# First two weight blocks computed together, input block by input block, and the first token group left unnormalised

## The chip, the cores and the metric

The kernel runs on one core of a Trainium2 chip. The metric is the device time of one launch in microseconds (us), the median of several runs. One run was also taken with the hardware profiler. The engines are named as the profile names them: PE (TensorE, matmuls; PEld its weight loads), DVE (VectorE), ACT (ScalarE), POOL (GpSimd) and SP (SyncE, which issues nearly all transfers).

## What is computed

One layer of a decoder for 2048 prompt tokens and 8 sequences of 8 sample tokens (2112 tokens in all), width 1024, in float32:

```
h    = rmsnorm(x) * norm_mix_w                       # one factor per token, rs = rsqrt(mean(x*x) + eps)
proj = h @ w_in                                      # 1024 x 4096: rq rk rv rg | hq hf hi hg, 4 heads of 128 each
o_r  = retention(rotary(rq), rotary(rk), rv)         # chunkwise, decay per head
o_h  = hgrn2(silu(hq), f(hf), hi)                    # chunkwise, decay per element from the forget gate f
o    = concat(head_rmsnorm(o_r)*silu(rg), head_rmsnorm(o_h)*silu(hg))
x    = x + o @ w_out
x    = x + square(relu(rmsnorm(x) @ w_up)) @ w_down
y    = rmsnorm(x)                                    # and the final states of both recurrences
```

The factor `rs` is one number per token, so a product of unnormalised tokens with the weights, multiplied by `rs` behind the product, is the same value as the product of normalised tokens.

## The kernel before

Tokens are kept transposed, 128 channels by tokens. They are mixed in three groups (`GROUPS`: 640, 768 and 704 tokens); the two recurrences of a group are worked head by head (`mix`), and a second phase, the MLP, follows for the whole. Only the start of the first group matters here.

Every float32 operand of a product is split into a high part in PE's fp32r type (`hi`, an ACT copy) and the rest (`lo`, a DVE subtraction). A product is three matmuls, hi-hi, hi-lo and lo-hi. With 640 tokens the group has two `pieces` of 320 columns. A projection block is 128 output channels: 8 input blocks (`KB`) x 3 x 2 pieces = 48 matmuls of 320 columns into two PSUM banks. A weight unit (`unit`, 128x1024) holds the eight 128x128 weights of one such block.

PSUM is split into two pools of four banks: `pj` for projections and `mm` for the mixing work. The order of the small work is laid down by an agenda: `at` and `later` put functions on it, and `tick` runs what is due each time `matmul` has issued a certain number of columns. `flush` runs the whole agenda.

`norm_start` reads the first group's 8 input blocks (`x_block`, 128x640) and splits `x * norm_mix_w` into hi and lo; there `rs` is not applied. It computes the squares (L600), their sum (L603) and by `factor` (L647, L407, L408) the token factor `rs`. While `g.post` is true, `normed` multiplies products by `rs` (L760). In head 0 of this group (`start` in `project`), blocks hf and hq (`sg`, `z`) are copied out of PSUM unnormalised (`evacuated`, L782); block three (rq) and block four (rk) stay in PSUM until rotary products L843 take them with tables that hold `rs` already (L817); then come the two gate blocks, and `values`, which multiplies tokens (as the stationary side) by the value weights and copies them out (L875). Between these, `norm_rest` has all 8 input blocks scaled by `rs` (L705) and split once more (L708, L712); from `values` of head 0 on, the normalised blocks are used.

`norm_squares`, for the next group, reads the next group's input into `ld` buffers (`ld<-x`, 128x768). It runs on the agenda of head 3, but its four first reads need nothing but free buffers, and they stand near the front of SP's queue.

Of the kernel before, what the change touches and what calls it, by code (L numbers as in the profile page):

```python
# [27 lines left out]
C = 128  # L28
# [24 lines left out]
W_BP = 0  # L53
# [141 lines left out]
class Kernel:  # L195
# [187 lines left out]
            out.append(self.blocks.popleft())  # L383
        return out

    def proj(self, g, blocks, acts):

        if self.singles:
            out = [(self.bank()[:, :c1 - c0], c0, c1) for c0, c1 in g.pieces]
# [227 lines left out]
    def norm_start(self, g):  # L617

        nc, T = self.nc, g.T
        self.starts(g)  # L620
        g.post, g.x = True, []
        for kb in range(KB):
            x, hi, lo = self.x_block(g, kb, True), self.getr(), self.getr()
            if kb == 0:
                self.ahead = 0
                self.unit(0)
            w = self.vec[:, V_MIX + kb:V_MIX + kb + 1]
            nc.scalar.activation(hi[:, :T], x[:, :T], AF.Copy, scale=w)
            nc.vector.scalar_tensor_tensor(out=lo[:, :T], in0=x[:, :T], scalar=w, in1=hi.bitcast(F32)[:, :T],
                                           op0=ALU.mult, op1=ALU.subtract)  # L630
            g.h.append((hi, lo))
            g.x.append(x)
        part = [None, None]

        def square(kb):
            part[kb % 2] = self.add_square(g, part[kb % 2], g.x[kb], nc.vector)

        def both():
            g.sq = part[0]
            nc.vector.tensor_tensor(out=g.sq[:, :T], in0=g.sq[:, :T], in1=part[1][:, :T], op=ALU.add)  # L640

        def factor():
            g.rs, ln = self.get(), self.get()
            for c0, c1 in g.pieces:
                sl = slice(c0, c1)
                ps = self.mm(c1 - c0)
                nc.tensor.matmul(ps, self.ones, g.sq[:, sl], start=True, stop=True)  # L647
                self.rsqrt(g.rs[:, sl], ps, ln[:, sl], self.eps, D)

        for kb in range(KB):  # L650
            self.at(24 + 2 * kb, square, kb)
        self.at(24 + 2 * KB, both)
        self.later(0, self.tables, g)
        self.later(60, factor)

    def norm_rest(self, g):

        t = dict(enumerate(g.x))
        self.plan_apply(g, t, lambda kb: None, 2, 5)
        g.x = None  # L660

    def norm_squares(self, g):
        self.starts(g)
# [56 lines left out]
    def mix(self, g, nxt):  # L720
        nc = self.nc
        if g.ns:
            g.qm = [self.get(), self.get()]
            for q in g.qm:
                nc.gpsimd.memset(q, 0.0)
        g.o, g.oc = {}, {}
        prev = None
        for p in range(H):
            b = {}
            gates = self.gates(g, p - 1, prev) if p > 1 else ()  # L730
            if p == H - 1 and nxt is not None:
# [10 lines left out]
            if p == 0 and g.post:  # L742
                g.post, g.h = False, [g.h_next[kb] for kb in range(KB)]
# [59 lines left out]
    def project(self, g, p, b, gates=()):  # L803
        nc, T = self.nc, g.T

        start = p == 0 and g.post
        if start:
            sg, z = self.evacuated(g, self.block(g)), self.evacuated(g, self.block(g))
            pj = self.block(g)
            xs = self.swapped(g, pj)  # L810
            self.fetch(self.con, self.I["con"])
            self.flush()
            self.masks()
            self.ordered = False
            cos, sin = self.get(), self.get()
            for scaled, table in ((sin, g.sin), (cos, g.cos)):
                nc.vector.tensor_tensor(out=scaled[:, :T], in0=table[:, :T], in1=g.rs[:, :T], op=ALU.mult)  # L817
            sg, z = self.normed(g, sg), self.normed(g, z)
            self.norm_rest(g)
        else:  # L820
            sg, z = self.two(g)
            cos, sin = g.cos, g.sin
        f, k = self.get(), self.get()
        sgq, hq = self.get(), self.get()
        self.sigmoids((sg[:, :T], sg[:, :T]), (sgq[:, :T], z[:, :T]), *((e[4][:, :T], e[3][:, :T]) for e in gates))
        self.gated(g, gates)
        b["f"], b["k"], b["q"] = f, k, hq

        def forget():
            nc.vector.tensor_scalar(out=f[:, :T], in0=sg[:, :T], scalar1=self.a1[:, p:p + 1], scalar2=self.lb[:, p:p + 1],  # L830
                                    op0=ALU.mult, op1=ALU.add)
            nc.gpsimd.tensor_scalar(out=k[:, :T], in0=sg[:, :T], scalar1=self.na1[:, p:p + 1], scalar2=self.a1[:, p:p + 1],
                                    op0=ALU.mult, op1=ALU.add)
        self.later(3, forget)
        self.later(3, lambda: nc.vector.tensor_tensor(out=hq[:, :T], in0=z[:, :T], in1=sgq[:, :T], op=ALU.mult))

        for i, key in enumerate(("rq", "rk")):
            if not start or key == "rk":
                pj = self.block(g)
                xs = self.swapped(g, pj)  # L840
            q = self.get()
            for ps, c0, c1 in pj:
                nc.vector.tensor_tensor(out=q[:, c0:c1], in0=ps, in1=cos[:, c0:c1], op=ALU.mult)  # L843
            nc.vector.tensor_tensor(out=xs[:, :T], in0=xs[:, :T], in1=sin[:, :T], op=ALU.mult)
            self.later(5, lambda q=q, xs=xs: nc.vector.tensor_tensor(out=q[:, :T], in0=q[:, :T], in1=xs[:, :T], op=ALU.add))
            b[key] = q

    def values(self, g, p, b):

        nc = self.nc  # L850
        w = [self.next_unit(), self.next_unit()]
        b["vs"], b["vc"] = None, []

        for i0 in range(0, len(g.starts), 4):
            part = g.starts[i0:i0 + 4]
            pj = [self.bank() for _ in range(0, len(part), 2)]
            vs = [self.get() for _ in range(0, len(part), 2)]
            for i, s in enumerate(part):
                cut = slice(i % 2 * 256, i % 2 * 256 + 256)
                for kb in range(KB):  # L860
                    hh, hl = g.h[kb]
                    cols = slice((kb % 4) * 256, (kb % 4 + 1) * 256)
                    wh, wl = w[kb // 4][0][:, cols], w[kb // 4][1][:, cols]
                    for q, (a, ww) in enumerate(((hh, wh), (hh, wl), (hl, wh))):
                        self.matmul(pj[i // 2][:, cut], a[:, s:s + C], ww, start=kb == 0 and q == 0,
                                    stop=kb == KB - 1 and q == 2)
                v = vs[i // 2]
# [5 lines left out]
                if i % 2 or i == len(part) - 1:  # L873
                    with self.soon():
                        nc.scalar.copy(v[:, :cut.stop], pj[i // 2][:, :cut.stop])  # L875

    def sample_states(self, which, h):
        out = []
# [927 lines left out]
```

## Time and profile before

| | us |
|---|---|
| runs | 2540.51, 2545.43, 2553.95; median 2545.43 |
| profiled execution | 2539.36 |
| its span | 2537.6 |
| PE busy in the span | 2497.3 (98%) |
| DVE busy | 1857.1 (73%) |
| ACT busy | 1231.8 (49%) |

A row of a timeline gives start, length (both us from the span's start), engine, line of the kernel, operation, output and input tiles, shapes and count, and in brackets how long the engine idled before it and what ended that. Grouped rows give busy us and the mean ns of one instruction. In both the buffer's number is left out of the names: `slab` is any of 49 buffers of 128x768, `w` a weight part, `raw` a weight as loaded.

### The profile page before, as it was taken

The page shows a single profiled execution, that of the slowest core. Times are in us where ns is not written, and L with a number is a line of the kernel's source. Part 1 is how long each engine was busy: PE and PEld are TensorE (multiplying, and loading weights), DVE is VectorE, ACT ScalarE, POOL GpSimd, SP SyncE. Part 2 cuts the span into 40 slices and gives each one's busy share as a digit, 9 for nine tenths or more (in the row PEclk, how much of TensorE's full clock was granted, in tenths as well). Part 3 has the DMA queues.
Part 4 walks back from the last instruction along what each step waited for, and adds up shares of the span by engine and source line. Part 5 has one row for each costly group of instructions (what it writes and reads, how often), then busy time and mean ns, then how long its engine had stood idle before and what let it go on. Part 6 is the DMA issues. An engine that isn't in the chain of part 4 may idle for free.

```text
span 2537.6 us, 41663 instructions
## 1 busy us (share of the span) xinstructions
PE 2497.3 (98%) x16600; PEld 2472.2 (97%) x16600; DVE 1857.1 (73%) x2737; ACT 1231.8 (49%) x1788; POOL 22.1 (1%) x42
## 2 busy tenths in 40 slices
PE   7999999999999999999999999999999999999998
PEld 7999999999999999999999999999999999999998
DVE  6767866677867756655666997766599866758987
ACT  5555754445534445425444543554454445445544
POOL 0000000000000000000000000000000000000000
PEclk9999999999999999999999999999999999999999
DMA  5556685787798844485667655566766554667652
GB/s 188 166 177 216 222 318 175 241 297 272 260 327 310 301 134 146 128 288 184 184 201 251 229 188 159 186 179 191 224 233 220 175 193 155 186 192 244 205 181 71
DMA packets 184435, 532.83 MB, mean 210 GB/s; under 512 B 20656, under 2 KB 44976, under 8 KB 184240
## 3 DMA queue, kind: packets, MB, share of 16 engines
q1 hardware_dynamic: 184096, 530.14, 62.8%
q8 instruction: 131, 2.15, 0.3%
q14 instruction: 64, 0.52, 0.1%
q10 hardware_dynamic: 144, 0.02, 0.0%
HBM read 390.62 MB, written 138.67 MB: 209 GB/s over the span
## 4 chain that ended last, share of the span: by engine, by line
PE 92%; DVE 3%; DMA 3%; ACT 1%; issue 1%; SPq 0%; DVEq 0%; ACTq 0%
PE pj L1329 84%; PE mm L1026 2%; PE po L1208 1%; PE mm L1214 1%; PE po L1206 1%; PE mm L1083 1%; DMA raw<-w 1%; PE mm L582 1%; PE mm L583 1%; DMA slab<-x 1%; PE mm L1140 1%; PE mm L956 0%; PE po L897 0%; DMA s68S<-raw 0%; DVE slab L987 0%
## 5 line engine op out<-in xcount | busy, mean ns | idle before, releaser
L1329 PE MATMUL pj<-slab,w 128*128 128x352 f32 (+2 forms) x12744 | 2114.9, 324 | 18.7 <-ACT w L335 5.9
L1329 PEld LDWEIGHTS pj<-slab,w 128*128 128x128 f32 x12744 | 2036.4, 188 | 24.9 <-ACT w L335 5.9
L338 ACT CAST w<-raw 128x1024 fp32r<-128x1024 f32 x374 | 392.2, 1049 | 617.8 <-PE pj L1329 524.8
L360 DVE TENSOR_TENSOR w<-raw,w 128x1024 fp32r<-128x1024 f32 x374 | 456.3, 1222 | 128.4 <-ACT w L338 118.6
L1329 PE MATMUL pj<-w,slab 128*128 128x256 f32 x1632 | 224.8, 287 | 1.0 <-DVE slab L760 1.0
L1377 DVE TENSOR_TENSOR slab<-slab 128x704 fp32r<-128x704 f32 x216 | 187.6, 886 | 31.3 <-ACT slab L1373 27.7
L1329 PEld LDWEIGHTS pj<-w,slab 128*128 128x128 f32 x1632 | 205.1, 190 | 2.5 <-DVE slab L760 1.2
L1373 ACT CAST slab<-slab 128x704 fp32r<-128x704 f32 x216 | 163.0, 778 | 91.2 <-DVE slab L1384 86.3
L1593 DVE TENSOR_TENSOR slab<-pj,slab 128x704 f32<-128x704 f32 x166 | 146.9, 888 | 62.2 <-PE pj L1329 60.9
L296 DVE TENSOR_TENSOR raw<-raw 128x1024 f32<-128x1024 f32 x60 | 73.4, 1224 | 47.7 <-DMA raw<-w 42.3
L1384 DVE TENSOR_TENSOR slab<-slab 128x704 f32<-128x704 f32 x120 | 103.6, 885 | 0.0
L1521 DVE TENSOR_TENSOR ld<-pj,slab 128x704 f32<-128x704 f32 x63 | 56.1, 890 | 53.6 <-PE pj L1329 53.5
L1007 ACT ACTIVATE slab<-slab 128x640 f32<-128x640 f32 (+2 forms) x72 | 56.2, 781 | 69.6 <-DVE slab L1003 69.2
L1521 DVE TENSOR_TENSOR slab<-pj,slab 128x704 f32<-128x704 f32 x42 | 37.4, 891 | 64.9 <-PE pj L1329 64.9
L1027 DVE COPY_PREDICATED AT<-msk,mm 128x256 f32<-128x256 uint8 (+1 forms) x72 | 38.7, 544 | 44.0 <-PE mm L1026 33.0
L762 ACT COPY slab<-pj 128x384 f32<-128x384 f32 (+2 forms) x88 | 35.6, 454 | 50.1 <-PE pj L1329 48.0
L401 ACT CAST slab<-slab 128x704 fp32r<-128x704 f32 (+2 forms) x48 | 37.0, 778 | 38.1 <-DMA slab<-o 16.0
L407 ACT ACTIVATE slab<-mm,eps 128x384 f32<-128x384 f32 (+3 forms) x54 | 29.5, 551 | 52.2 <-PE mm L583 50.3
L1026 PE MATMUL mm<-slab 128*128 128x128 f32 x384 | 54.1, 274 | 0.0
L1026 PEld LDWEIGHTS mm<-slab 128*128 128x128 f32 x384 | 51.1, 191 | 0.0
L1208 PE MATMUL po<-slab,S 128*128 128x128 f32 x240 | 46.3, 279 | 4.5 <-DVE S L1221 4.5
L775 ACT COPY slab<-pj 64x320 f32<-64x320 f32 (+2 forms) x48 | 21.6, 450 | 56.4 <-PE pj L1329 38.1
(177 smaller groups left out, 1971.8 us busy)
## 6 DMA issues: line engine op xcount, KB each, us to landing
raw<-w SPq DMA_DIRECT2D x254, 512.0 KB, 4.3
u<-ld SPq DMA_DIRECT2D x96, 352.0 KB, 4.3
slab<-u SPq DMA_DIRECT2D x96, 352.0 KB, 5.0
y<-slab SPq DMA_DIRECT2D x20, 352.0 KB, 2.9
ld<-x SPq DMA_DIRECT2D x16, 384.0 KB, 7.0
raw<-s44S SPq DMA_DIRECT2D x12, 512.0 KB, 3.6
raw<-s48S SPq DMA_DIRECT2D x12, 512.0 KB, 4.4
raw<-s52S SPq DMA_DIRECT2D x12, 512.0 KB, 3.8
```

The costliest lines, as they stand in the source:

```text
L296: nc.vector.tensor_tensor(out=x[into], in0=x[a], in1=x[b], op=op)
L338: self.nc.scalar.copy(hi, raw)
L360: self.nc.vector.tensor_tensor(out=lo, in0=raw, in1=hi.bitcast(F32), op=ALU.subtract)
L1007: nc.scalar.activation(x["dd", w][:, a:T], x["dd", w][:, a:T], AF.Exp)
L1026: nc.tensor.matmul(ps[:, j * P:(j + 1) * P], qk[:, cols[c]], qk[:, cols[c]], start=True, stop=True)
L1208: nc.tensor.matmul(dst, S, qd[:, cols[c]], start=False, stop=True)
L1329: self.nc.tensor.matmul(out, w, a, **k)
L1373: self.nc.scalar.copy(hi[:, :g.T], B[name][:, :g.T])
L1377: self.nc.vector.tensor_tensor(out=lo[:, :g.T], in0=B[name][:, :g.T], in1=hi.bitcast(F32)[:, :g.T], op=ALU.subtract)
L1384: self.nc.vector.tensor_tensor(out=s[:, :g.T], in0=B[a][:, :g.T], in1=B[b][:, :g.T], op=op)
L1521: nc.vector.tensor_tensor(out=b2(out), in0=ps, in1=b2(s), op=ALU.add)
L1593: nc.vector.tensor_tensor(out=r, in0=ps, in1=r, op=ALU.add)
```

## The change

The first two weight units no longer come as wholes: they are read in four quarters of 128x256 each, a pair of quarters behind every second input block, and split quarter by quarter. `first_pair` multiplies each arriving input block by both weight blocks, into all four `pj` banks. Block three goes into two `mm` banks; blocks three and four are copied out of PSUM by ACT. `norm_rest` is gone: the group's tokens stay unnormalised in all four heads. So the rotary tables are scaled by `rs` in place once, every evacuation of a projection block of the group multiplies by `rs` on DVE, and `values` multiplies its rows by `rc`, the factor by rows (five 128x128 transposes, `factor_columns`), on ACT, once for each 256 columns.

```
+    def first_pair(self, g):
+        out = [[(self.bank()[:, :c1 - c0], c0, c1) for c0, c1 in g.pieces] for _ in range(2)]
+        for kb, (ah, al) in enumerate(g.h):
+            cut = slice(kb * P, kb * P + P)
+            for j in range(2):
+                wh, wl = (t[:, cut] for t in self.wts[j])
+                for q, (w, a) in enumerate(((wh, ah), (wh, al), (wl, ah))):
+                    for ps, c0, c1 in out[j]:
+                        self.matmul(ps, w, a[:, c0:c1], start=kb == 0 and q == 0, stop=kb == KB - 1 and q == 2)
+        return [self.evacuated(g, pj) for pj in out]
...
     def norm_start(self, g):
+        def weights(q):
+            cut = slice(q * 256, q * 256 + 256)
+            for j in range(2):
+                self.fetch(raws[j][:, cut], self.I["w"][W_BP + j][:, cut])
...
-            if kb == 0:
-                self.ahead = 0
-                self.unit(0)
+            if kb % 2 == 0:
+                weights(kb // 2)
...
-            self.at(24 + 2 * kb, square, kb)
-        self.at(24 + 2 * KB, both)
+            self.at(14 + 3 * kb, square, kb)
+        self.at(14 + 3 * KB, both)
...
-        self.later(60, factor)
+        self.later(46, factor)
...
     def project(self, g, p, b, gates=()):
-            sg, z = self.evacuated(g, self.block(g)), self.evacuated(g, self.block(g))
-            pj = self.block(g)
+            sg, z = self.first_pair(g)
+            pj = self.evacuated(g, self.proj(g, self.take(KB), g.h, self.mm))
...
-            self.norm_rest(g)
...
-                pj = self.block(g)
+                pj = self.evacuated(g, self.block(g)) if start else self.block(g)
...
     def values(self, g, p, b):
+        if g.post and p == 0:
+            self.factor_columns(g)
...
+                if g.post:
+                    with self.soon():
+                        nc.scalar.activation(v[:, cut], pj[i // 2][:, cut], AF.Copy, scale=g.rc[:, i0 + i:i0 + i + 1])
```

How SP's queue stands at the start, before. `slab<-x` are the input blocks of this group, `raw<-w` weights, `ld<-x` the next group's input:

```order
L225 DMA slab<-x 128x640
L225 DMA raw<-w 128x512 x2
L225 DMA raw<-w 128x1024 x4
L225 DMA slab<-x 128x640
L225 DMA ld<-x 128x768 x3
L225 DMA slab<-x 128x640
L225 DMA ld<-x 128x768
L225 DMA slab<-x 128x640 x5
```

The same place now:

```order
L225 DMA slab<-x 128x640
L225 DMA raw<-w 128x256 x2
L225 DMA ld<-x 128x768 x2
L225 DMA slab<-x 128x640
L225 DMA ld<-x 128x768 x2
L225 DMA slab<-x 128x640
L225 DMA raw<-w 128x256 x2
L225 DMA slab<-x 128x640 x2
L225 DMA raw<-w 128x256 x2
L225 DMA slab<-x 128x640 x2
L225 DMA raw<-w 128x256 x2
L225 DMA slab<-x 128x640
```

Only quarters of the first two weights stand between the input blocks; the whole weights that follow have moved behind the last input block, and the four `ld` reads have moved up.

PE from the start to the first value products (`pj<-w,slab`), before:

```order
L1329 MATMUL pj<-slab,w 128x320 x167
L647 MATMUL mm<-slab,ones 128x320 x2
L1329 MATMUL pj<-slab,w 128x320 x121
L582 MATMUL mm<-slab,ones_r 128x256
L582 MATMUL mm<-slab,ones_r 128x384
L583 MATMUL mm<-slab,ones_r 128x256
L583 MATMUL mm<-slab,ones_r 128x384
L1329 MATMUL pj<-w,slab 128x256 x11
```

And now (L677 is what L647 was, L594 and L595 what L582 and L583 were):

```order
L1365 MATMUL pj<-slab,w 128x320 x96
L1365 MATMUL mm<-slab,w 128x320 x48
L1365 MATMUL pj<-slab,w 128x320 x23
L677 MATMUL mm<-slab,ones 128x320 x2
L1365 MATMUL pj<-slab,w 128x320 x100
L594 MATMUL mm<-slab,ones_r 128x256
L1365 MATMUL pj<-slab,w 128x320 x6
L594 MATMUL mm<-slab,ones_r 128x384
L1365 MATMUL pj<-slab,w 128x320
L595 MATMUL mm<-slab,ones_r 128x256
L595 MATMUL mm<-slab,ones_r 128x384
L1365 MATMUL pj<-slab,w 128x320 x14
```

The counts are the same, 288 products ahead of the values, and the factor's matmul stands behind 167 in both; block three has moved to `mm` banks, and the own sums have moved into the last gate block. Five transposes (L910) follow.

ACT between the last input block (L656) and the factor (L419), now:

```order
L656 ACTIVATE slab<-slab,vec 128x640
L338 CAST w<-raw 128x1024 x3
L612 ACTIVATE slab<-slab 128x640 x7
L804 COPY slab<-pj 128x320 x4
L612 ACTIVATE slab<-slab 128x640
L338 CAST w<-raw 128x1024
L419 ACTIVATE slab<-mm,eps 128x320
```

Before, one weight copy (L338) and the first two evacuations (L782, now L804) stood ahead of the squares (L600, now L612); now three weight copies and seven squares stand ahead of all four evacuations.

More of the change, by code (lines that the diff above doesn't have):

```diff
@@ L384, in take, with proj @@
         return out
-    def proj(self, g, blocks, acts):
+    def first_pair(self, g):
[8 more added lines that the diff above has]
+        return [self.evacuated(g, pj) for pj in out]
+    def proj(self, g, blocks, acts, bank=None):
         if self.singles:
-            out = [(self.bank()[:, :c1 - c0], c0, c1) for c0, c1 in g.pieces]
+            out = [((bank or self.bank)()[:, :c1 - c0], c0, c1) for c0, c1 in g.pieces]
         else:
@@ L621, in norm_start, with weight_parts @@
         g.post, g.x = True, []
+        raws = [self.raw_tile() for _ in range(2)]
+        for j in range(2):
+            self.wts[j] = self.w_tile(), self.w_tile()
+        self.w_load = self.w_next = self.w_use = 2
+        def weights(q):
+            cut = slice(q * 256, q * 256 + 256)
+            for j in range(2):
+                self.fetch(raws[j][:, cut], self.I["w"][W_BP + j][:, cut])
+        def weight_parts(q):
+            cut = slice(q * 256, q * 256 + 256)
+            for j in range(2):
+                hi, lo = self.wts[j]
+                nc.scalar.copy(hi[:, cut], raws[j][:, cut])
+                nc.vector.tensor_tensor(out=lo[:, cut], in0=raws[j][:, cut], in1=hi.bitcast(F32)[:, cut], op=ALU.subtract)
         for kb in range(KB):
             x, hi, lo = self.x_block(g, kb, True), self.getr(), self.getr()
-            if kb == 0:
-                self.ahead = 0
-                self.unit(0)
+            if kb % 2 == 0:
+                weights(kb // 2)
             w = self.vec[:, V_MIX + kb:V_MIX + kb + 1]
@@ L630, in norm_start @@
                                            op0=ALU.mult, op1=ALU.subtract)
+            if kb % 2 == 0:
+                weight_parts(kb // 2)
             g.h.append((hi, lo))
@@ L650, in norm_start @@
         for kb in range(KB):
-            self.at(24 + 2 * kb, square, kb)
-        self.at(24 + 2 * KB, both)
+            self.at(14 + 3 * kb, square, kb)
+        self.at(14 + 3 * KB, both)
         self.later(0, self.tables, g)
-        self.later(60, factor)
[L656 to L660, printed above, removed]
+        self.later(46, factor)
     def norm_squares(self, g):
@@ L741, in mix @@
                 self.open_gates(g, self.gates(g, p, b))
-            if p == 0 and g.post:
-                g.post, g.h = False, [g.h_next[kb] for kb in range(KB)]
             if p == H - 1:
@@ L814, in project @@
             self.ordered = False
-            cos, sin = self.get(), self.get()
-            for scaled, table in ((sin, g.sin), (cos, g.cos)):
-                nc.vector.tensor_tensor(out=scaled[:, :T], in0=table[:, :T], in1=g.rs[:, :T], op=ALU.mult)
+            for table in (g.sin, g.cos):
+                nc.vector.tensor_tensor(out=table[:, :T], in0=table[:, :T], in1=g.rs[:, :T], op=ALU.mult)
+            cos, sin = g.cos, g.sin
             sg, z = self.normed(g, sg), self.normed(g, z)
-            self.norm_rest(g)
         else:
@@ L872, in values, with factor_columns @@
                     b["vc"].append(pair)
-                if i % 2 or i == len(part) - 1:
+                if g.post:
+                    with self.soon():
+                        nc.scalar.activation(v[:, cut], pj[i // 2][:, cut], AF.Copy, scale=g.rc[:, i0 + i:i0 + i + 1])
+                elif i % 2 or i == len(part) - 1:
                     with self.soon():
                         nc.scalar.copy(v[:, :cut.stop], pj[i // 2][:, :cut.stop])
+    def factor_columns(self, g):
+        nc = self.nc
+        g.rc = self.mp.tile([P, KB], F32, name="rc")
+        for i0 in range(0, len(g.starts), 4):
+            part = g.starts[i0:i0 + 4]
+            ps = self.mm(len(part) * P)
+            for i, s in enumerate(part):
+                nc.tensor.transpose(ps[:, i * P:(i + 1) * P], g.rs[:, s:s + C], self.ident)
+            nc.vector.tensor_copy(g.rc[:, i0:i0 + len(part)], ps.rearrange("p (i t) -> p i t", t=P)[:, :, 0])
     def sample_states(self, which, h):
```

## The prediction

> **What bounds the kernel now.** I read the page first, then the table of busy time by stretches, then TensorE's (PE's) timeline at the start, and last what PE waits for there.
>
> ```profile
> PE 2497.3 (98%) x16600; PEld 2472.2 (97%) x16600; DVE 1857.1 (73%) x2737; ACT 1231.8 (49%) x1788; POOL 22.1 (1%) x42
> PE   7999999999999999999999999999999999999998
> 0.00:30.64 30.64, 19.17 (x97) 17.04 (x97) 12.58 (x25) 12.64 (x17) 2.27 (x12) 1.00 0.78 279
> 30.64:49.78 19.14, 15.42 (x100) 14.86 (x101) 14.38 (x19) 15.46 (x26) 0.79 (x1) 1.00 0.42 148
> 49.78:69.15 19.37, 17.20 (x100) 16.22 (x100) 19.24 (x33) 10.57 (x16) 0.21 (x1) 0.91 0.10 28
> 69.15:88.82 19.67, 19.67 (x177) 19.13 (x178) 18.29 (x37) 13.07 (x22) 0.00 (x0) 1.00 0.26 82
> ```
>
> PE is the bound: it idles 2537.6 - 2497.3 = 40.3 us in all, and of these 11.5 + 3.7 + 2.2 = 17.4 lie in the first 69.15 us (first columns of the stretches: length, PE, PE weight load, VectorE (DVE), ScalarE (ACT), POOL; then granted clock, DMA share, GB/s). From 69.15 on PE has no gap, so the change can win only ahead of that. DVE is full (19.24 of 19.37) just before it.
>
> ```profile
> 5.93 2.10 PE L1329 MATMUL pj<-slab,w 128*128 128x320 f32 x6 [5.93 <-ACT w L335]
> 8.63 2.16 PE L1329 MATMUL pj<-slab,w 128*128 128x320 f32 x6 [0.60 <-ACT w L338]
> 15.08 14.97 PE L1329 MATMUL pj<-slab,w 128*128 128x320 f32 x84 [4.29 <-ACT slab L628]
> 30.64 10.68 PE L1329 MATMUL pj<-slab,w 128*128 128x320 f32 x71 [0.58 <-ACT slab L782]
> 41.16 1.24 PE L647 MATMUL mm<-slab,ones 128*128 128x320 f32 x4
> 49.78 16.10 PE L1329 MATMUL pj<-slab,w 128*128 128x320 f32 x96 [3.73 <-DVE slab L843]
> 65.89 0.56 PE L582 MATMUL mm<-slab,ones_r 128*128 128x256 f32 x2
> 67.61 0.55 PE L583 MATMUL mm<-slab,ones_r 128*128 128x256 f32 x2 [1.16 <-DVE slab L402]
> 69.15 1.57 PE L1329 MATMUL pj<-w,slab 128*128 128x256 f32 x11 [0.98 <-DVE slab L760]
> ```
>
> The rows are start, length, what, count, and the wait ahead. Before 69.15 stand six blocks of 48 products: the first two (6 + 6 + 84), blocks three and four up to 46 us, the two gate blocks at 49.78; then value products begin. Without waits a product takes 10.68 / 71 = 0.150 us, and the six 288 x 0.150 = 43.2; with L647, L582 and L583 it is 45.6. So 69.15 - 45.6 = 23.6 us are waits and slow products: the ceiling of any gain.
>
> ```profile
> 8.07 0.43 SPq L225 DMA_DIRECT2D slab<-x  x1
> 14.20 0.83 ACT L628 ACTIVATE slab<-slab,vec 128x640 fp32r<-128x640 f32 x1 [4.34 <-DMA slab<-x]
> 18.84 10.95 PEld L1329 LDWEIGHTS pj<-slab,w 128*128 128x128 f32 x72 [0.47 <-ACT slab L628]
> 19.76 4.14 ACT L628 ACTIVATE slab<-slab,vec 128x640 fp32r<-128x640 f32 x5 [0.98 <-DMA slab<-x]
> 0.00:4.00 4.00, 0.00 (x0) 0.00 (x0) 0.60 (x5) 1.28 (x1) 2.27 (x12) 1.00 0.56 161
> 4.00:8.00 4.00, 2.07 (x6) 1.50 (x6) 3.22 (x11) 2.52 (x5) 0.00 (x0) 1.00 0.99 325
> 8.00:12.00 4.00, 2.19 (x7) 1.54 (x6) 2.45 (x2) 1.63 (x2) 0.00 (x0) 1.00 0.88 298
> 12.00:16.00 4.00, 0.92 (x3) 0.77 (x3) 0.89 (x1) 0.83 (x1) 0.00 (x0) 1.00 0.98 349
> raw<-w SPq DMA_DIRECT2D x6, 512.0 KB, 6.6
> slab<-x SPq DMA_DIRECT2D x8, 320.0 KB, 7.1
> ld<-x SPq DMA_DIRECT2D x4, 384.0 KB, 7.4
> ```
>
> Three causes. First, the second input block is only issued at 8.07, behind 2.5 MB of weights, and is used at 14.20; the last one is ready at 23.9 (transfers above: count, KB each, us to landing; they run at about 300 to 350 GB/s).
>
> ```profile
> 43.37 0.47 ACT L408 ACTIVATE slab<-slab 128x320 f32<-128x320 f32 x1
> 43.88 1.56 DVE L817 TENSOR_TENSOR slab<-slab 128x640 f32<-128x640 f32 x2 [3.00 <-ACT slab L408]
> 49.15 0.88 DVE L843 TENSOR_TENSOR slab<-pj,slab 128x320 f32<-128x320 f32 x2
> L705 DVE SCALAR_TENSOR_TENSOR slab<-slab,vec 128x640 f32<-128x640 f32 x8 | 6.8, 880 | 0.0
> L712 DVE TENSOR_TENSOR slab<-slab 128x640 fp32r<-128x640 f32 x8 | 6.6, 821 | 0.0
> 48.00:52.00 4.00, 2.20 (x8) 2.03 (x9) 4.00 (x8) 3.96 (x6) 0.99 (x1) 0.77 0.02 4
> 52.00:56.00 4.00, 4.00 (x24) 4.00 (x23) 3.87 (x7) 2.53 (x6) 0.00 (x0) 0.80 0.00 0
> ```
>
> Second, the gates wait 3.73 us for PSUM banks that only L843 frees, which needs the token factor (ready at 43.84); the granted clock falls to 0.77 and 0.80 behind that gap, so 96 products take 16.10 instead of 14.4. Third, DVE works through L705 and L712, the normalised copies, and value products wait for them.
>
> **The change, part by part.** The start. Now the first two weight blocks come in quarters between the input blocks. Up to the last input block SP's queue carries 8 x 320 + 8 x 128 + 4 x 384 = 5120 KB, 5.24 MB (the four `ld` loads of the next group stay in front). At the rows' rates 0.64 MB are in at 4.0 us and 4.53 at 16.0; the rest at 349 GB/s takes 2.0: last block in at about 18, ready some 2 us later (0.83 for its ACT copy, the rest my allowance for landing). PE's own pace: the second block has 1.70 MB up to its end, in at 7.3, usable at about 9. From there stand 84 products. Early products are slow: the 12 from 15.08 to 18.84 took 3.76, less 0.47 of waiting, 0.27 each; after 18.84 they are at 10.95 / 72 = 0.15. With 12 to 24 slow ones it is 14 to 15.5 us and ends at 23 to 24.5. I take 24 for the start of block three, against 30.64: **6.6 us gained**. Bounds: 22 (transfers alone plus the last 12 products) and 27 (48 of the 84 products slow).
>
> ```profile
> L338 ACT CAST w<-raw 128x1024 fp32r<-128x1024 f32 x5 | 5.3, 1055 | 9.2 <-PE pj L1329 9.2
> L600 ACT ACTIVATE slab<-slab 128x640 f32<-128x640 f32 x8 | 5.3, 744 | 0.0
> L782 ACT COPY slab<-pj 128x320 f32<-128x320 f32 x4 | 1.5, 427 | 0.0
> ```
>
> Block three writes other banks (`mm`), so it doesn't wait for the pair's copies. Block four does: ACT ahead of it has two weight copies that wait for the pair's end (2 x 1.05), seven squares (7 x 0.66 = 4.6) and two copies (0.8), 7.5 us, against block three's 48 x 0.15 = 7.2. A stall of 0.3, taken as 0 to 1.
>
> The middle. Behind block three's start stand 192 products x 0.150 = 28.8, L647 1.24, the two own sums 1.1. The gates no longer wait for L843: ACT copies blocks three and four out (4 x 0.43 = 1.7, on an engine with 8.8 us free in the third stretch). The 16 instructions of L705 and L712 (13.4 us of DVE) and eight ACT casts are gone. What is late next is the same DVE chain without them. The factor comes after 48 + 23 products and 2.7 us (41.16 to 43.84), at 24 + 10.7 + 2.7 = 37.4. From 43.88 to 69.15 DVE took 25.3, of which seven L705 and six L712, about 11, leave 14.3: it ends at 51.7. PE reaches L583 after 178 products, 1.24 and some 0.4, at 24 + 28.3 = 52.3. So PE waits 0 to 1 here, and DVE is close behind: nothing more is to be had in the middle. New on PE are five transposes for the factor by rows.
>
> ```profile
> 85.87 0.49 PE L956 MATMUL mm<-con,slab 128*128 128x128 f32 x3
> L760 DVE TENSOR_TENSOR slab<-pj,slab 128x320 f32<-128x320 f32 x4 | 1.8, 482 | 0.0
> L762 ACT COPY slab<-pj 128x320 f32<-128x320 f32 x24 | 8.9, 424 | 1.4 <-PE pj L1329 1.4
> 89.00:130.00 41.00, 40.99 (x303) 40.77 (x303) 25.65 (x54) 24.95 (x40) 0.88 (x1) 1.00 0.69 231
> ```
>
> By L956 they take 5 x 0.16 = 0.8. Values then start at 24 + 28.8 + 1.24 + 1.1 + 0.8 + 0.5 of stalls = 56.4 against 69.15. The second term is 38.5 - 32.4 = **6.1**, bounds 4 to 7.
>
> Later heads of the group. 24 copies from PSUM (L762) become DVE products at L760's 0.48: 11.6 us more on DVE, beside PE while DVE is 25.65 of 41 busy. Value copies on ACT become five scaled ones instead of three, on ACT with 16 of 41 free. Cost on the path: 0, at worst 1 to 2 if an evacuation comes late. Behind this group the order is the old one, all shifted.
>
> Sum: 6.6 + 6.1 = **12.7**. The profiled execution took 2539.36 (span 2537.6) and would take 2526.7. The median shown is 2545.43, 6 us above it: 2532.7.
>
> **A rule against it.** PE's clock in the rows: 0.27 a product early, 0.15 after 18.84, and 0.77 granted behind the 3.73 us gap. The Trainium skill, "TensorE: Matmul & The Clock Gate", Part 1: the clock starts at half, needs a full busy window of about 3.4 us to rise, and an idle window halves it again. The trace agrees (a gap of 3.73, half speed behind it). It speaks against feeding products piece by piece: by it gaps between input blocks could hold the clock down throughout the pair. By the one the pair ends at 24, by the other as in the first rival.
>
> **Rivals.** *The pair stays slow.* All 96 products at 0.27, 25.9 us from 5.93, end at 31.8: the first term is -1.2, the gain 4.9 and the time 2540.5. For it: the first 12 products now also come in pieces with 4.29 between. Against it: two blocks share each input, so PE has 12 products per arrival instead of 6 and the waits shrink. Half of it (an end at 27 to 28) gives 2536. Chance 0.13.
>
> *DVE holds the values.* If the factor's chain runs as before though L705 and L712 are gone, for it also waits on ACT's sigmoids and copies (22 instead of 14.3), values start near 60.5 and the gain is 8.6: 2537. For it: DVE has no slack in the third stretch. Against: eight ACT casts leave too. Chance 0.13.
>
> *Slower.* DVE's extra 24 evacuations hold PE's banks. A bank is wanted again one block later, 7.2 us after its block ends; a DVE backlog above that stops PE. Twelve blocks at 2.2 us each (a backlog of 9.4) cost 26.4, less 12.7: 2559. It decides from 1.1 us each on. Against: DVE is 63% busy there. Chance 0.04.
>
> *More.* Transfers at over 400 GB/s and a clock up after 12 products, pair done at 21.5: gain 15 to 17, 2529. Chance 0.20.
>
> **How the numbers follow.** The forecast, a gain of 11 to 14.5, 2531 to 2534.5, has 0.50. A measurement of this kernel tells about 0.5% (12.7 us, 2532.7) from no change, and my value lies on that edge. Faster by over 0.5%: the last rival and half of the forecast's share, 0.45. Within: the other half and the first two rivals, 0.51. Slower: 0.04. The range 2523 to 2542 goes from the best start to the slow pair, with 5 us at the lower end (the ceiling of 23.6 is 2522) and 1.5 at the upper for the spread of the runs.
>
> **What would show it.** Block three starts at 22 to 27; no gap in front of the gates, and granted clock 1.00 from 20 us on; values start at 54 to 58; L705 and L712 absent and DVE below full in that stretch; the heads behind without PE gaps. Wrong would be a pair beyond 28, a wait at L583 over 2 us, or PE waiting for DVE's evacuations.

## The result and the profile after

| | before | after |
|---|---|---|
| median of 8 runs, us | 2545.48 (2540.51 to 2553.95) | 2533.44 (2528.67 to 2537.13) |
| ratio | | 0.9953, 95% interval 0.9939 to 0.9966 |
| profiled execution, us (span) | 2539.36 (2537.6) | 2532.16 (2530.4) |

The gain is 12.0 us. The page's first line, and the busy times of PE, PE's weight load, DVE, ACT and POOL in the four stretches that answer to those of before:

```profile
PE 2498.1 (99%) x16605; PEld 2472.6 (98%) x16605; DVE 1855.8 (73%) x2750; ACT 1223.8 (48%) x1769; POOL 26.4 (1%) x42
0.00:24.45 24.45, 17.75 (x97) 17.05 (x97) 12.48 (x29) 12.14 (x20) 2.27 (x12) 1.00 0.89 304
24.45:35.70 11.25, 11.25 (x78) 11.01 (x76) 8.92 (x10) 8.68 (x16) 0.00 (x0) 1.00 0.81 304
35.70:55.54 19.84, 19.28 (x132) 18.91 (x131) 17.60 (x31) 14.45 (x22) 3.15 (x1) 1.00 0.18 54
55.54:75.21 19.67, 19.60 (x175) 18.62 (x174) 14.79 (x32) 12.72 (x23) 0.00 (x0) 1.00 0.25 82
```

PE's busy time is what it was; its idle time up to the value products fell from 17.4 us to 6.70 + 0.56 = 7.3. PE's timeline from the start to the values:

```profile
5.82 3.84 PE L1365 MATMUL pj<-slab,w 128*128 128x320 f32 x12 [5.82 <-ACT w L648]
10.54 14.07 PE L1365 MATMUL pj<-slab,w 128*128 128x320 f32 x84 [0.88 <-ACT slab L656]
24.45 7.20 PE L1365 MATMUL mm<-slab,w 128*128 128x320 f32 x48
31.49 3.54 PE L1365 MATMUL pj<-slab,w 128*128 128x320 f32 x23
34.86 1.24 PE L677 MATMUL mm<-slab,ones 128*128 128x320 f32 x4
35.70 15.07 PE L1365 MATMUL pj<-slab,w 128*128 128x320 f32 x100
52.63 0.56 PE L595 MATMUL mm<-slab,ones_r 128*128 128x256 f32 x2 [0.56 <-DVE slab L414]
55.08 0.71 PE L910 MATMUL mm<-con,slab 128*128 128x128 f32 x5
55.54 2.03 PE L1365 MATMUL pj<-w,slab 128*128 128x256 f32 x15
```

Block three starts at 24.45 (before: 30.64), the gates follow block four without a gap (before: 3.73 us of waiting and 16.10 for 96 products), and the values start at 55.54 (before: 69.15). That is a lead of 13.6 us. It does not last to the end. To follow it, matmuls of the two kernels are counted from the last one backwards, and starts with the same number are compared. "Values" is the lead at the first value product; the other two columns are the lead where the kernel before stands at 120.3 us (in head 1) and at 331.6 us (behind the first group's heads):

| kernel | block three, us | values, us | lead at values | at 120 | at 331 |
|---|---|---|---|---|---|
| changed | 24.45 | 55.54 | 13.6 | 13.0 | 10.8 |
| changed, again | 25.24 | 56.33 | 12.8 | 12.2 | 10.0 |
| loops exchanged | 24.48 | 55.57 | 13.6 | 12.9 | 10.8 |
| start alone | 24.18 | 62.91 | 6.2 | 3.8 | 3.8 |
| middle alone | 32.02 | 63.91 | 5.2 | 4.6 | 2.5 |
| pair apart | 28.51 | 58.79 | 10.4 | 9.7 | 7.6 |
| heads without the factor | 24.48 | 55.58 | 13.6 | 12.9 | 12.9 |
| values without the factor | 24.10 | 55.20 | 14.0 | 13.3 | 13.0 |
| `ld` held back | 21.82 | 52.92 | 16.2 | 15.6 | 11.9 |
| the same, PE warm | 20.44 | 51.53 | 17.6 | 17.0 | 13.2 |
| values by DVE | 23.75 | 54.84 | 14.3 | 13.7 | 12.8 |
| all three | 20.73 | 51.83 | 17.3 | 16.7 | 12.3 |
| before, again | 31.10 | 69.60 | -0.45 | -0.45 | -0.45 |

Every kernel with the changed middle loses 0.6 us between the values and 120 (the start alone, with the old middle, loses 2.4 there to its clock, below). The changed kernel then loses 2.1 more in heads 1 to 3.

### The profile page after: what moved, and what is told of

Read it like the earlier page. It is cut to its first block, busy times and chain, and to the rows that moved or that the text cites. A ratio compares the mean times of both kernels' runs of the same rounds, so it can differ in the third digit from the quotient of the medians.

```text
span 2530.4 us, 41661 instructions
## 1 busy us (share of the span) xinstructions
PE 2498.1 (99%) x16605; PEld 2472.6 (98%) x16605; DVE 1855.8 (73%) x2750; ACT 1223.8 (48%) x1769; POOL 26.4 (1%) x42
## 4 chain that ended last, share of the span: by engine, by line
PE 93%; DMA 2%; DVE 2%; ACT 1%; issue 1%; SPq 0%; DVEq 0%; ACTq 0%
PE pj L1365 84%; PE mm L1062 1%; PE po L1244 1%; DMA raw<-w 1%; PE mm L1250 1%; PE po L1242 1%; PE mm L1119 1%; PE mm L595 1%; PE mm L594 1%; DMA s44S<-raw 1%; PE mm L1176 1%; PE po L933 1%; PE mm L992 1%; DVE slab L1023 0%; PE mm L1365 0%
## 5 line engine op out<-in xcount | busy, mean ns | idle before, releaser
L338 ACT CAST w<-raw 128x1024 fp32r<-128x1024 f32 x373 | 391.5, 1050 | 611.3 <-PE pj L1365 515.2
L360 DVE TENSOR_TENSOR w<-raw,w 128x1024 fp32r<-128x1024 f32 x373 | 455.0, 1222 | 116.3 <-ACT w L338 103.9
L1413 DVE TENSOR_TENSOR slab<-slab 128x704 fp32r<-128x704 f32 x216 | 187.6, 886 | 31.1 <-ACT slab L1409 27.5
L1557 DVE TENSOR_TENSOR ld<-pj,slab 128x704 f32<-128x704 f32 x63 | 56.1, 890 | 53.6 <-PE pj L1365 53.4
L1557 DVE TENSOR_TENSOR slab<-pj,slab 128x704 f32<-128x704 f32 x42 | 37.4, 891 | 64.9 <-PE pj L1365 64.9
L419 ACT ACTIVATE slab<-mm,eps 128x384 f32<-128x384 f32 (+3 forms) x54 | 29.6, 551 | 52.8 <-PE mm L595 49.6
L784 ACT COPY slab<-pj 128x384 f32<-128x384 f32 (+1 forms) x64 | 26.7, 466 | 49.4 <-PE pj L1365 47.3
L1327 ACT ACTIVATE slab<-po 128x384 f32<-128x384 f32 (+2 forms) x48 | 22.0, 459 | 56.4 <-PE po L1244 56.3
```

Source lines behind the costliest of these rows:

```text
L338: self.nc.scalar.copy(hi, raw)
L360: self.nc.vector.tensor_tensor(out=lo, in0=raw, in1=hi.bitcast(F32), op=ALU.subtract)
L1413: self.nc.vector.tensor_tensor(out=lo[:, :g.T], in0=B[name][:, :g.T], in1=hi.bitcast(F32)[:, :g.T], op=ALU.subtract)
L1557: nc.vector.tensor_tensor(out=b2(out), in0=ps, in1=b2(s), op=ALU.add)
```

## The experiments

Medians beside each other, each with its ratio to the kernel before on the same chip. The intervals of the ratios reach 3 to 7 us to each side, and those of the changed versions overlap or touch throughout. So the lead in the trace up to 331 us, not the median, tells kernels of this family apart.

| kernel | median, us | before, us | ratio (95%) |
|---|---|---|---|
| changed, again | 2537.9 | 2549.35 | 0.9947 (0.9932 to 0.9962) |
| start alone | 2539.81 | 2549.35 | 0.9963 (0.9947 to 0.9980) |
| middle alone | 2542.14 | 2549.35 | 0.9969 (0.9956 to 0.9983) |
| loops exchanged | 2533.7 | 2549.35 | 0.9937 (0.9918 to 0.9956) |
| heads without the factor | 2534.65 | 2545.91 | 0.9953 (0.9936 to 0.9969) |
| `ld` held back | 2537.89 | 2545.91 | 0.9955 (0.9938 to 0.9972) |
| pair apart | 2536.71 | 2545.91 | 0.9961 (0.9942 to 0.9979) |
| before, again | 2546.37 | 2545.91 | 1.0005 (0.9992 to 1.0018) |
| values without the factor | 2531.05 (one run) | 2552.61 | |
| `ld` held back, PE warm | 2540.97 | 2552.61 | 0.9952 (0.9929 to 0.9975) |
| values by DVE | 2536.06 | 2552.61 | 0.9937 (0.9911 to 0.9963) |
| all three | 2536.32 | 2552.61 | 0.9939 (0.9918 to 0.9960) |

**The start alone.** The pair, the quarters and block three's banks as in the change; the tokens are normalised again, and blocks three and four stay in PSUM.

```
             sg, z = self.first_pair(g)
-            pj = self.evacuated(g, self.proj(g, self.take(KB), g.h, self.mm))
+            pj = self.proj(g, self.take(KB), g.h, self.mm)
...
+            self.norm_rest(g)
```

> Only the start of the change: the first two weights in quarters, the pair computed together input block by input block, block three in mm banks; tokens are still normalised behind the factor (norm_rest) and used normalised from the values of head 0 on, as before. My theory (start and middle gain apart and add): the pair ends at about 24.5 us as in the changed kernel, the factor is ready some 6 us earlier than the 43.8 of before, and the values, which still wait for VectorE's normalised copies, start at about 63 instead of 69.15: 6 us faster than before (2 runs' medians, 5 to 7). Rival (VectorE holds the values whatever the start does, since the normalised copies fill it): values within 2 us of 69, no gain beyond 2 us. Rival (the start is the whole gain): 10 us or more.

PE's timeline of this run behind block four:

```profile
49.52 7.30 PE L1359 MATMUL pj<-slab,w 128*128 128x320 f32 x48 [2.99 <-DVE slab L873]
59.35 0.57 PE L594 MATMUL mm<-slab,ones_r 128*128 128x256 f32 x2 [2.52 <-ACT slab L413]
61.38 0.64 PE L595 MATMUL mm<-slab,ones_r 128*128 128x256 f32 x2 [1.46 <-DVE slab L414]
62.91 2.72 PE L1359 MATMUL pj<-w,slab 128*128 128x256 f32 x11 [0.90 <-DVE slab L790]
```

Block three starts at 24.18, and 6.2 us of lead are left at the values: from block three to there it takes 38.7 us, as before (38.5). The gates run at full clock here (7.30 for 48 products), but that gains nothing, since PE then waits longer for the sums and the values (2.52, 1.46 and 0.90, before 0, 1.16 and 0.98). Behind these waits the trace grants half clock from 61.7 to 68.5, later than in the kernel before (50.2 to 53.6) and twice as long; that takes 2.4 of the 6.2 back. Heads 1 to 3 lose nothing.

**The middle alone.** The old start, and blocks three and four copied out, `norm_rest` gone, the factor behind the products.

```
-            pj = self.block(g)
+            pj = self.evacuated(g, self.block(g))
...
-            self.norm_rest(g)
...
+        if g.post and p == 0:
+            self.factor_columns(g)
```

> Only the rest of the change: the start is that of before (two whole weights ahead of the inputs, blocks one after the other), tokens stay unnormalised in the group, blocks three and four are copied out of PSUM by ScalarE. My theory: block three starts at 30.6 us as before, no wait ahead of the gates, values start some 31.5 us later, at 62, 7 us ahead of before; about 2.5 us of it are lost again in heads 1 to 3, where the group's remainder took 253.8 us in the changed kernel against 250.9 before, so 4 to 5 us faster than before in all. Rival (nothing is lost later, the traces differ by their own waits): 7 us faster. Rival (the middle is hidden anyway): no gain.

From block three to the values it takes 31.9 instead of 38.5: 6.6 us gained. One wait remains there:

```profile
59.94 0.39 PE L595 MATMUL mm<-slab,ones_r 128*128 128x256 f32 x1 [1.23 <-DVE slab L414]
63.91 1.68 PE L1347 MATMUL pj<-w,slab 128*128 128x256 f32 x12
```

The lead is 5.2 and not 6.6 because this run's block three started 1.4 later than in the profile before. It loses 2.1 us in heads 1 to 3, as the changed kernel does: the loss belongs to the middle's edit.

**The loops of the pair exchanged.** Block one ahead of block two in the code, with nothing to hold that order.

```
-            for j in range(2):
+        for j in range(2):
+            for kb, (ah, al) in enumerate(g.h):
```

> The changed kernel with its loads in quarters as they are, but the first block computed over all input blocks before the second (the two loops of first_pair exchanged). My theory (a shared arrival halves the waits): the first block ends with the last input, at about 21.7 us, the second 48 x 0.147 = 7.1 us later, block three starts at about 28.7 instead of 24.45, and the kernel is 4 us slower than the changed one (8 faster than before). Rival (the order of the loads alone gives the gain): same as the changed kernel, within 1 us.

PE does 12 products on the first input block all the same (its first row is x12, as in the changed kernel), so this is another run of that order: block three at 24.48 and a lead of 10.8 at 331. The next kernel pins the order.

**The changed kernel again.**

> The changed kernel once more, beside the others on this chip: 12 us faster than before by the medians. Its trace tells which of the later waits change from run to run: if the 3.3 us wait near 448 us and the 1.8 us wait near 794 us of the first trace are the run's own, they differ here.

Block three at 25.24, the lead at 331 is 10.0. Two runs of one kernel differ by 0.8 us at the start; their loss in heads 1 to 3 agrees (2.1 and 2.1).

**The pair apart.** The first block's 48 products ahead of the second's, held in that order.

```
+        self.pinned = True
+        for j in range(2):
+            for kb, (ah, al) in enumerate(g.h):
...
+        if self.pinned:
+            self.tc.keep_in_program_order(i)
```

> The changed kernel with the first weight block's 48 products ahead of the second's 48, and everything else as it is. Theory one (computing the pair together is what fills PE between the input blocks): the second block's 48 products begin only when the last input block is there (19 to 20 us) and take 7.2, block three starts at 27 to 28.5, and the time is 3 to 4 us above the changed kernel's. Theory two (the gain at the start comes from the quarters of the weights alone, which bring the input blocks earlier): block three starts at 24 to 25 and the time is the same within 1 us.

PE's timeline at the start:

```profile
10.72 2.36 PE L1368 MATMUL pj<-slab,w 128*128 128x320 f32 x6 [2.82 <-ACT slab L659]
13.77 14.90 PE L1368 MATMUL pj<-slab,w 128*128 128x320 f32 x84 [0.69 <-ACT w L651]
28.51 7.20 PE L1368 MATMUL mm<-slab,w 128*128 128x320 f32 x48
```

Block three starts at 28.51, 4.1 us later: PE waits for input blocks it could have used twice. The clock has a small part in this: full clock is granted from 18.5 us on here and from 13.8 in the changed kernel. But the last input block is ready only at 19.7, and 54 products of 0.147 us must follow it, so by this estimate block three could not start before 27.7 even with an early clock. So of the 6.2 us of the start, 3.2 to 4.1 are the pairing, and the rest of the start's edit (the quarters, and what stands where in the queue) gives 2 to 3 (30.64 to 28.51 in this run).

**The `ld` reads held back.** The four reads of the next group's input go back to their place in the code, so that 4 x 384 KB leave the front of the queue.

```
         def load(kb):
+            self.ordered = g.i == 1
             x[kb] = self.x_block(g, kb)
+            self.ordered = False
```

> The changed kernel with the four ld reads of the next group's input held back to their place in the code, so that the queue carries 1.57 MB less up to the last input block. Theory one (transfers set the end of the first pair): at 300 to 350 GB/s the last input block comes 4 to 5 us earlier, is ready at 15 to 16 us instead of 19.8, block three starts at 20.5 to 22.5 instead of 24 to 25, and the time is 2 to 3 us below the changed kernel's. Theory two (PE's half clock and its 96 products set the end): block three starts at 23.5 to 25 and the time is the changed kernel's within 1 us.

```profile
5.64 16.34 PE L1367 MATMUL pj<-slab,w 128*128 128x320 f32 x96 [5.64 <-ACT w L648]
21.82 7.20 PE L1367 MATMUL mm<-slab,w 128*128 128x320 f32 x48
52.92 2.04 PE L1367 MATMUL pj<-w,slab 128*128 128x256 f32 x15
```

The 96 products now run without a gap, and block three starts 2.6 us earlier. The clock rose earlier too, at 9.8 us instead of 13.8, but that is not the gain: with the loops exchanged and the `ld` reads in front it rose at 9.2, and PE waited 1.23 and 0.81 us for early pieces instead and started block three at 24.48. So transfers did hold up the pair, by its early pieces. The lead at 120 us is 15.6. By 331 it falls to 11.9, by 3.7 where the changed kernel loses 2.1, and the time is the changed kernel's. The place where the further 1.6 goes:

```profile
256.81 0.45 PE L594 MATMUL mm<-slab,ones_r 128*128 128x384 f32 x1
258.29 0.44 PE L595 MATMUL mm<-slab,ones_r 128*128 128x384 f32 x1 [1.03 <-DVE slab L589]
259.15 2.90 PE L1367 MATMUL pj<-slab,w 128*128 128x320 f32 x18 [0.43 <-DVE slab L866]
```

A sum of head 2 waits for its split on DVE (L589). This wait is in no kernel whose `ld` reads stand early, and in all three with the reads held back. In these three DVE's order is another: a weight subtraction (L360, 1.23 us) stands right ahead of the split, which starts at 257.68 here; in the changed kernel the split comes before it, at 256.79.

**The same, with PE warm.** 16 matmuls of the `ones` tile ahead of the first product.

```
+        warm = self.mm(P)
+        for _ in range(16):
+            self.nc.tensor.matmul(warm, self.ones, self.ones, start=True, stop=True)
```

> The changed kernel with the ld reads held back, and 16 matmuls of the ones tile with itself (128x128, result unused) on PE ahead of the first product, from about 1.1 us on. Theory one (with the transfers out of the way PE's half clock up to 9.8 us is what is left): the clock is up by 6 to 8 us, the products wait for the pieces instead, the last 72 start at about 9.9 and take 10.8, block three starts at 20.5 to 21 instead of 21.8, about 1 us gained. Theory two (gaps between the first pieces take the clock down again, or the pair is bound otherwise): block three starts at 21.5 to 24.

```profile
1.05 5.46 PE L653 MATMUL mm<-ones 128*128 128x128 f32 x32 [1.05 <-DVE eps L456]
6.27 14.33 PE L1370 MATMUL pj<-slab,w 128*128 128x320 f32 x96
20.44 7.20 PE L1370 MATMUL mm<-slab,w 128*128 128x320 f32 x48
```

The 96 products take 14.33 instead of 16.34, though they begin 0.6 later; block three starts 1.4 earlier. With the transfers out of the way, the half clock was what was left: full clock is granted from 4.5 us on here, from 9.8 without the warm-up, and no gap between pieces took it down again.

**Heads without the factor.** This kernel leaves the factor out in heads 1 to 3: the evacuations are ACT copies there, and the values are copied unscaled, two pieces at a time.

```
-                if g.post:
+                if g.post and self.head0:
...
-                if g.post:
+                if g.post and p == 0:
```

> Left out: the token factor on the products of heads 1 to 3 of the first group (head 0 keeps it). There the evacuations are ACT copies again and the value copies go two 256-column pieces at a time without a scale, and PE's order in these heads is that of the kernel before. Theory one (the 2.9 us that the changed kernel loses between 81 and 331 us comes from what the factor costs in heads 1 to 3: DVE evacuations, scaled value copies, and the order that they bring): PE's lead over the kernel before stays within 0.5 us from the first value products to the end of the group, and the time is 2.5 to 3 us below the changed kernel's, a ratio of 0.9935 to 0.9945 to the kernel before. Theory two (the loss is one of runs, or of the early start itself): the lead falls by 2 to 3 us as in the changed kernel, and the time is the same as the changed kernel's within 1 us.

The lead stays at 12.9 from 120 to 331 us. So the factor costs 2.1 us there. The expected 2.9 take in the 0.6 of head 0, which this kernel leaves as it is.

**Values without the factor.** Only the second of the two edits above.

> Left out: the factor on the values of heads 1 to 3 of the first group, whose copies therefore go two 256-column pieces at a time (three ACT copies a head where the changed kernel has five). The evacuations stay DVE products with the factor. PE's order in these heads is that of the kernel before. Theory one (the five value copies, by the waits and the order that they bring, cost the 2.1 us that the changed kernel loses between 120 and 331 us): the lead over the kernel before stays at 12.5 to 13 us, as with the factor left out altogether. Theory two (the 24 evacuations on DVE cost it): the lead falls by 1.5 to 2.5 us, as in the changed kernel.

The lead is 13.3 at 120 and 13.0 at 331, with the DVE evacuations in place. Those cost at most 0.3; the value copies cost the rest. PE at the same place of head 1, in the changed kernel and then here:

```profile
114.78 0.71 PE L1365 MATMUL pj<-w,slab 128*128 128x256 f32 x4
115.75 0.38 PE L594 MATMUL mm<-slab,ones_r 128*128 128x256 f32 x1 [0.26 <-ACT slab L419]
115.98 0.27 PE L595 MATMUL mm<-slab,ones_r 128*128 128x256 f32 x1
116.09 0.38 PE L1242 MATMUL po<-slab 128*128 128x128 f32 x2
116.31 0.39 PE L1242 MATMUL po<-AT,slab 128*128 128x128 f32 x2
116.45 0.36 PE L1365 MATMUL pj<-w,slab 128*128 128x256 f32 x1
116.81 0.71 PE L1250 MATMUL mm<-slab 128*128 128x128 f32 x4
```

```profile
114.44 0.95 PE L1365 MATMUL pj<-w,slab 128*128 128x256 f32 x6
115.40 0.39 PE L594 MATMUL mm<-slab,ones_r 128*128 128x256 f32 x1
115.63 0.28 PE L595 MATMUL mm<-slab,ones_r 128*128 128x256 f32 x1
115.75 1.83 PE L1365 MATMUL pj<-w,slab 128*128 128x256 f32 x14
117.42 0.39 PE L1242 MATMUL po<-slab 128*128 128x128 f32 x2
```

With five scaled copies the scheduler puts L594 two value products earlier and draws L1242 and L1250 forward. L594 then waits for ACT (L419), and only 1 and 7 value products stand between the small ones, where 14 stood in a row. From here to the next long run of value products it takes 4.24 us (114.78 to 119.02); the same instructions take 3.9 in the other kernel (114.44 to 119.78, less 12 value products of 0.12). The same rows come back at 189 us in head 2. They make up some 0.3 us each time; by the lead, the changed kernel loses 0.5 in head 1, 0.7 in head 2 and the rest in head 3, and the other places were not followed row by row. That five copies cost 2.1 us is shown; that they do it by PE's order is read from these rows, as no run held the old order with five copies.

**Values by DVE.** Nothing left out: in heads 1 to 3 one DVE product evacuates two pieces and multiplies by the factor by rows.

```
+                if g.post and p:
+                    if i % 2 or i == len(part) - 1:
...
+                        nc.vector.tensor_tensor(out=v..., in0=pj..., in1=g.rc[:, j:j + w2]..., op=ALU.mult)
```

> The changed kernel, with the values of heads 1 to 3 copied out two pieces at a time by one DVE product with the factor by rows (three DVE products a head instead of five scaled ACT copies). PE's order in these heads is that of the kernel before; nothing is left out. Theory one (the five ACT copies cost the 2.1 us): the lead stays at 12.5 to 13 us up to 331 us and the time is about 2 us below the changed kernel's, a ratio of 0.994 to 0.995. Theory two (DVE's extra work costs it): the lead falls by 2 to 4 us and the time is the changed kernel's or above.

The lead is 13.7 up to 252 us of the kernel before and 12.8 at 331: of the 2.1 us, 1.2 come back. The largest wait behind that point is one for DVE, in head 3:

```profile
303.00 0.68 PE L1068 MATMUL mm<-slab 128*128 128x128 f32 x4 [0.36 <-DVE AT L1069]
```

**All three edits.**

> All three edits on the changed kernel: ld reads held back, 16 matmuls of ones ahead, values of heads 1 to 3 by DVE in pairs. Theory one (the gains add): block three at 20.5 to 21, value products at 51.5 to 52, a lead of 16 to 17 us over the kernel before that holds to 331 us instead of 10.8 in the changed kernel, and a time 4 to 6 us below the changed kernel's, a ratio of 0.9925 to 0.9935. Theory two (an earlier PE meets later limits that don't move, such as the transfers of the next group and the state products near 447 us): the lead is given back by 550 us and the time is the changed kernel's within 2 us, a ratio of 0.9945 to 0.996.

At 120 the lead is 16.7 and it holds up to 252 us of the kernel before; the first theory's 16 to 17 is met that far. Then half clock follows the wait that the held-back `ld` brings (257.7 to 261.1 us), and 18 products that took 2.90 above take 4.44:

```profile
256.00 0.44 PE L595 MATMUL mm<-slab,ones_r 128*128 128x384 f32 x1 [1.04 <-DVE slab L589]
256.87 4.44 PE L1376 MATMUL pj<-slab,w 128*128 128x320 f32 x18 [0.43 <-DVE slab L869]
```

At 331 it is 12.3. By its ratio, 0.9939, it is not told from the changed kernel; no version here is shown to beat it.

**The kernel before, again.**

> The kernel before, once more, for a second profile and as a measure of what two sets of runs of one kernel differ by. Expected: a ratio of 1.000 within 0.0015; block three at 30.5 to 31.5 and the value products at 69 to 70 us. If the waits of 1 to 3.3 us that the changed kernel shows at 448 and 794 us, and the products that take 161 instead of 159 ns in part of the second phase, belong to single runs, this profile has some of them elsewhere or not at all; if they belong to the change, it has neither.

Its trace agrees with the profile before to 0.5 us up to 331 us. It has the wait near 459 as well (below); the wait at 794 it hasn't.

## Why the prediction was right

The time, 2532.7, stands 0.7 us from the median, and the gain, 12.7, inside its interval (0.34% to 0.61%, 9 to 15.5 us). That it came so near is in part luck: the profiled execution was put at 2526.7 and took 2532.16, and two errors in the sum cancel in part. Step by step:

- *Block three at 24.* It started at 24.45; the first term is 6.2 instead of 6.6. The working was two bounds that met: transfers, and 84 products with 12 to 24 slow ones. Both were real. In this run it was the clock: 12 of the 84 lie ahead of 13.85, where full clock is granted, and the other 72 take 10.6 us. Where the clock came earlier, waits for pieces took its place. Holding back 1.5 MB gives 2.6 us and a warm PE 1.4 on top. The first rival, a pair kept slow by gaps between its pieces, did not come: in the rows of the changed kernel the gap is 0.88 us, and from 13.85 on the products run at full pace. Apart, with gaps of 2.82, the pair was 4.1 later, as the step said of 12 products per arrival instead of 6. The last rival, transfers at over 400 GB/s, did not come either: the first stretch has 304 GB/s.
- *A stall at block four, 0 to 1.* None: 31.49 follows 24.45 by 7.04.
- *The middle, 6.1 with bounds of 4 to 7.* It is 38.5 - 31.1 = 7.4, above the bound. The places were right: no gap at the gates, half clock gone, one wait for L414 of 0.56. The sizes were a little high, since row lengths were added where starts count: the products go by 0.147 (71 from 24.45 to 34.86), not 0.150; L677 is 1.24 long but the next row starts 0.84 behind it; the transposes take 0.46, not 0.8. Together 1.4 us.
- *DVE close behind.* It is busy 17.60 of 19.84 us where it was full, and the wait for it is 0.56: the second rival, DVE holding the values to 60.5, is out. (By the prediction's own numbers the values would then start at 62.3: the chain ends at 37.4 + 22 = 59.4, and 14 products and the transposes, 2.9 us, still follow.)
- *Later heads at 0, at worst 1 to 2.* This step is the one that failed, by 2.1 us in heads 1 to 3 and 0.6 in head 0. It priced the 24 evacuations that move to DVE, and these do cost almost nothing, at most the 0.3 above, so the third rival (slower, by DVE's evacuations) is out too:

```profile
L782 DVE TENSOR_TENSOR slab<-pj,slab 128x320 f32<-128x320 f32 x26 | 11.5, 485 | 7.4 <-PE pj L1365 7.2
L898 ACT ACTIVATE slab<-pj,rc 128x256 f32<-128x256 f32 x20 | 9.2, 467 | 8.0 <-PE pj L1365 8.0
```

These are groups of the changed kernel from 55.54 to 309; both engines idle ahead of them, waiting for PE. The prediction had the value copies on ACT as covered by ACT's free time. They cost PE 2.1 us, with another order of its work, and that had no term. That PE has no gap from 69.15 us on was read from a row that ends at 88.82; 22.9 of its 40.3 idle us lie behind 69.15. The order of the heads could have been read from the compiled kernel before any run.

The too small second term and the missing one cancel in part: 6.2 + 7.4 - 0.6 - 2.1 = 10.9, the lead of 10.8 at 331. That lies in the interval of the gain (9 to 15.5). The profiled pair shows less at its end, 7.2, since each execution goes its own way behind 331 us. The changed kernel's row and that of the kernel before, at the same product:

```profile
450.91 0.80 PE L1244 MATMUL po<-slab,S 128*128 128x128 f32 x2 [3.02 <-DVE S L1257]
```

```profile
460.88 0.49 PE L1208 MATMUL po<-slab,S 128*128 128x128 f32 x2 [2.18 <-DVE S L1221]
```

PE waits there in every run, for 0.9 to 3.3 us from product to product, and in some of them half clock follows, as at 450.8 to 454.2 here. That took 2.4 us of this profile's lead; in its second run the wait was 0.9. The 0.6 us of head 0 lie between its first value product and the next head's first product:

```profile
88.82 1.19 PE L1329 MATMUL pj<-slab,w 128*128 128x320 f32 x7
```

```profile
75.86 1.19 PE L1365 MATMUL pj<-slab,w 128*128 128x320 f32 x7
```

From 69.15 that is 19.67 us before, and from 55.54 it is 20.32 now, with hardly any wait of PE (busy 19.60 of 19.67 in the last stretch above) and the value products in other groups between the small ones. No run takes this apart.

## What to carry to other kernels

Where PE starves while transfers come in, give it two blocks' work per arrival: here that was worth 3.2 to 4.1 us of the start's 6.2. An operation that is split into more, smaller ones on an idle engine need not be free, since a scheduler may lay out the bound engine's work in another order for it: compare that order in every stage that the edit touches, not only at the place that the edit is for. When the gain is a few us in 2500, follow the lead product by product; medians of a dozen runs did not separate kernels that differ by 2 us at 331.

## What the runs showed that was not expected

In the second phase products run at two paces, both with a granted clock of 1.00: 631 or 623 in 100 us, 1.3% apart. The first row is the profile before, then two stretches of its second profile, then one of the kernel with PE warm (PE's busy time, the clock, DMA share and GB/s):

```profile
1300.00:1400.00 100.00, 100.00 (x632) 1.00 0.72 230
```

```profile
1300.00:1400.00 100.00, 100.00 (x631) 1.00 0.71 235
2300.00:2400.00 100.00, 100.00 (x623) 1.00 0.66 222
```

```profile
1300.00:1400.00 100.00, 100.00 (x623) 1.00 0.68 222
```

The kernel before shows both in one execution, so it is not the change. The second phase is three stretches of some 465 us, with bounds near 1610 and 2075 us. In the 14 profiles each stretch keeps one pace from 100 us behind its start to its end, and from stretch to stretch the pace changes in either direction; 21 of the 42 stretches have the lower one. By the leads it is worth some 5 us in one stretch, and in all three some 15, more than the change. The two profiles compared above, before and after, have it nowhere. Of the runs of the kernel with PE warm, three lie at 2526.0 to 2526.5 and nine from 2539.65 on; its profile, one of the nine, has the lower pace in all three stretches. What causes it stays open.

The moment at which PE first goes at full pace varied from run to run of one kernel. The trace's first record of the clock lies at 13.8 us in the changed kernel, 15.4 in its second run, and 9.2 with the loops exchanged, where PE's order is the same; there PE waited for transfers instead, and block three started at 24.48 all the same.

Half clock came by windows of fixed length. The half-clock stretches ahead of the last one are 3.413 us long or twice that, and a full stretch is a whole multiple: with all three edits it is 252.586 us, 74 times 3.413. The Trainium skill, "TensorE: Matmul & The Clock Gate", Part 1, describes it so: a free-running window of 3413 ns, half clock behind an idle window. The trace agrees on the window but not on how idle it must be: two waits of 1.04 and 0.43 us were enough with all three edits, while the same two (1.03 and 0.43) cost nothing with the `ld` reads held back alone, where by the count of windows the second reaches into the next one. The length of a wait does not decide it: near 449 us one of 2.32 (`ld` held back) was followed by half clock, and one of 2.71 (values without the factor) was not. What does decide stays open. The Trainium skill, "TensorE: Matmul & The Clock Gate", Part 1, has the first rise vary by 0.5 us from run to run under sustained matmuls; here, where PE waits for pieces in between, it varies by 6.2 (9.2 to 15.4).
